# Neighbourhood attention on one Trainium2 core: slots of scores, values, transposes and fill, splits on VectorE, queries by pairs of units, shared bias tables

## The chip, the cores and the metric

The kernel runs as one program on one core of a Trainium2 chip. The core has five engines that work side by side, each through its own instructions in order: TensorE (PE in the profile) multiplies matrices and transposes, VectorE (DVE) and ScalarE (ACT) work on elements, GpSimd (POOL) too, and SyncE (SP) mostly starts transfers. Sixteen DMA engines move the data between HBM and the on-chip memory. The metric is the time of one execution on the device in microseconds; less is better. The times before the change are those of three runs, with their median.

## The reference

One layer of a hybrid encoder: an adaptive RMSNorm, a projection whose columns go to two groups of heads (2-D neighbourhood attention, and a bidirectional mLSTM), an output projection, a gated residual and a last RMSNorm. There are 2048 tokens (a grid of 32 rows and 64 columns) of width 1024, in float32. Cut to what the change touches:

```python
def rmsnorm(x, w):
    x32 = x.astype(jnp.float32)
    return x32 * lax.rsqrt(jnp.mean(x32 * x32, axis=-1, keepdims=True) + EPS) * w

def neighbourhood_attention(q, k, v, rpb):      # 8 heads of 64, window of 8 rows x 16 columns
    ...
    bias = rpb[:, dy[:, None, :, None], dx[None, :, None, :]]
    s = jnp.einsum('bhrcd,bhrjkd->bhrcjk', qg, kg).astype(jnp.float32) + bias[None]
    s = jnp.where(col_mask[:, None, :], s, -jnp.inf)
    p = jax.nn.softmax(s.reshape(B, NA_HEADS, rows, GRID_W, kh * GRID_W), axis=-1).reshape(s.shape)
    o = jnp.einsum('bhrcjk,bhrjkd->bhrcd', p, vg)
    return o.transpose(0, 2, 3, 1, 4).reshape(B, T, NA_W)
...
    na_out = neighbourhood_attention(na_q, na_k, na_v, rpb) * jax.nn.silu(na_z)
    ...
    return jnp.concatenate([na_out, ml_out], axis=-1) @ w_out
...
        h_res = h_res + gate[:, None, :] * y
    return rmsnorm(h_res, final_norm_w).astype(x.dtype)
```

## The kernel before

`phase1` and `phase1b` come first: the conditioning, the first norm, the input projection and the mLSTM. They leave queries (`d_qna`, a high and a low part), values (`d_vna`), the gate (`d_zna`), the mLSTM's output (`d_mix`), the output weights times the gate (`d_wo`) and tables of bias and mask (`d_t`) in HBM. The change touches only `phase2`, L1181 to L1500, which does the attention, the output projection and the last norm.

**Patches and units.** The grid is cut into 16 patches of 8 rows by 16 columns, 128 queries each, taken column by column, up and down in turn. A patch looks at 264 to 480 keys, by its place (edge patches at fewer, inner ones at 480). A unit is a patch and a pair of heads `ct` (0 to 3), so there are 64. Each goes through four stages:

- `stage_s`: four matmuls make the scores of two heads into `pS` (L1302 with the high part of the queries, L1303 with the low part); VectorE adds the table and takes the minimum in one instruction into `pbuf` (L1309); ScalarE takes the exponential and its sum (L1310). Behind L1309 the next table is loaded (L1274).
- `stage_n`: VectorE's reciprocal (L1319) and two multiplications, the normalisation (L1321).
- `stage_t`: TensorE transposes the probabilities into `pT` (L1331), and ScalarE copies them to `pt` (L1333).
- `stage_o`: TensorE multiplies by the values (`v` chunks of 4 or 5 grid rows) into `pO` (L1346), and VectorE multiplies by the gate, in `zs` or `gtile` by turns (L1348).

**The fill.** A generator, `outproj`, yields the 48 matmuls of a patch's output projection (L1376, into `y`), behind which VectorE adds x (L1381) and ScalarE squares (L1382). `pump(n)` takes n of them. In the first five slots the fill is what is left of the input projection (`pq`, L861). Matmuls in float32 precision go in three products of a high and a low part, so mixes and weights are split: `split_mix` and `split_w` make the high part on ScalarE (L1353, L1281) and the low part by a subtraction, most of them on GpSimd (L1354, L1282). `whi_a` and `wlo_a` hold the mixes of two patches by turns.

**The order.** It is written by hand. Slot n on TensorE is: values of unit n-2, transposes of n-1, scores of n, eight fill matmuls, four more. The normalisation of unit n is issued between the eight and the four, and is read by the transposes of the next slot. There are two `pbuf` tiles, one per head of the pair. What comes after a patch's projection (`last`: the rsqrt chain L1392 to L1178 and the scaling L1403, `store`, `load_x`) waits in the list `todo`, one entry a slot.

**The loads.** SP's queue issues tables, queries, values, gate and mixes in the order of the program; each waits for the readers of the tile that it fills, and for the SP load eight places before it, since eight semaphores go round. Queries come per patch: two of 256 KB (L1222) and two of 128 KB (L1229), at the patch's second unit, three slots ahead; one value chunk (L1243) at the third unit, the rest at the fourth, the gate (L1253) at the fourth. Tables have four buffers, two per unit. x loads (L1265) and output stores go through POOL's queue. In `phase2` SP issues 264 loads of queries, tables, values, gates and mixes: 64, 128, 40, 16 and 16.

Of the kernel before, what the change touches and what calls it, by code (L numbers as in the profile page):

```python
# [15 lines left out]
P = 128  # L16
# [7 lines left out]
NH = 8  # L24
# [34 lines left out]
class Kernel:  # L59
# [1121 lines left out]
    def phase2(self):  # L1181
# [29 lines left out]
        L = {b: {"tab": {}} for b in range(16)}  # L1211
        fnw = []

        qlow = [p.tile([P, NH, P], F32R, name=f"qlow{i}") for i in range(2)]
# [3 lines left out]
        def load_q2(b):  # L1218
            q2 = p.tile([P, NH, P], F32R, tag="q2", bufs=2, name=f"q2_{b}")
            src = self.d_qna[0, b].rearrange("(j p) c q -> p j (c q)", j=2)  # L1220
            for half in (q2[0:HD], q2[HD:P]):
                nc.sync.dma_start(half.bitcast(F32).rearrange("p (j c) q -> p j (c q)", j=2), src)  # L1222
            L[b]["q2"] = q2

        def load_ql(b):
            ql = qlow[pos[b] % 2]
            for j in range(2):
                js = slice(j * HD, (j + 1) * HD)
                nc.sync.dma_start(ql[js, 4 * j : 4 * j + 4, :].bitcast(F32), self.d_qna[1, b, js])  # L1229
            L[b]["ql"] = ql  # L1230

# [36 lines left out]
        NTAB = 4  # L1268

        def load_tab(i):  # L1270
            b, h = patches[i // 8], i % 8
            pr, pc, nr, nkc, nk, rpc, nch = geo[b]
            t = p.tile([P, 480], F32, tag="tab", bufs=NTAB, name=f"tab_{b}_{h}")
            nc.sync.dma_start(t[:, :nk], self.d_t[PR_T[pr]][PC_T[pc]][h])  # L1274
            L[b]["tab"][h] = t

# [8 lines left out]
        units = [(b, ct) for b in patches for ct in range(4)]  # L1285
        NU = len(units)
        U = {}

        def stage_s(u):
            b, ct = units[u]  # L1290
            pr, pc, nr, nkc, nk, rpc, nch = geo[b]
            lb = L[b]
# [5 lines left out]
            for j in range(2):  # L1298
# [3 lines left out]
                nc.tensor.matmul(o, lb["q2"][:, 4 * j + ct, :], kv, start=True, stop=False)  # L1302
                nc.tensor.matmul(o, lb["ql"][:, 4 * j + ct, :], kv, start=False, stop=True)  # L1303
                scores.append(ps)
            for j, ps in enumerate(scores):
                h = 2 * ct + j
                pt = pbuf[j]
                mn = p.tile([P, 1], F32, tag="mn", bufs=4, name=f"mn_{u}_{j}")
                nc.vector.tensor_tensor_reduce(pt[:, :nk], ps, lb["tab"].pop(h)[:, :nk], 1.0, 3e38, ALU.add, ALU.min, mn)  # L1309
                nc.scalar.activation(pt[:, :nk], pt[:, :nk], AF.Exp, bias=mn, scale=-1.0, accum_out=sums[:, j : j + 1])  # L1310
                pts.append(pt)
                if 2 * u + j + NTAB < 2 * NU:
# [256 lines left out]
```

## Time and profile before

| | us |
|---|---|
| median of 3 runs | 1469.06 |
| lowest, highest | 1464.5, 1472.09 |
| the profiled execution, own time | 1463.16 |
| its span in the trace | 1461.4 |
| first score matmul of the attention stage | 1020.5 |
| transposes' wait for the normalisation, in that stage | 25.5 |
| wait for values, in that stage | 17.9 |

The trace is of the profiled execution, so what is added to or taken from a time is added to 1463.16. The stage from 1020.5 to the end, some 441 us, is the one that the change touches; the first 1020 us are the same code in both kernels. "Busy" adds up the instructions' times on an engine. A window row gives for a stretch of the span the busy time and the count of each engine, then the clock granted to TensorE (1.00 is full), the mean busy share of the DMA engines, and GB/s. A row of waits reads: engine, tile and line that waited, what it waited for, total us, how many times, and the longest.

### The profile page before, as it was taken

What the parts mean: (1) busy time and instruction counts of PE and PEld (TensorE: products, weight loads), DVE (VectorE), ACT (ScalarE), POOL (GpSimd) and SP (SyncE); (2) the same over time, 40 slices, a digit from 0 to 9 for tenths busy, and PEclk for the clock granted to TensorE, in tenths of its full rate; (3) what the DMA queues carried; (4) which work ended last, traced back from release to release, by engine and by line L of the source; (5) the groups of instructions that cost most, each with busy time, mean ns of one, the idle gap of its engine ahead of it and who ended that gap; (6) DMA issues with size and microseconds to landing.
All of it is one profiled execution on the core that took longest, in us unless ns stands there. A gap on an engine that the chain in (4) does not pass through costs nothing.

```text
span 1461.4 us, 23327 instructions
## 1 busy us (share of the span) xinstructions
PE 1330.4 (91%) x8052; PEld 1133.7 (78%) x8052; DVE 791.5 (54%) x2487; ACT 527.4 (36%) x1119; POOL 285.0 (20%) x264
## 2 busy tenths in 40 slices
PE   3989998998999999999999999999779899799896
PEld 3889997998878787788788887777657677577675
DVE  6673332111464593467678787664335476466554
ACT  4633343442232232123232132223344355355451
POOL 4443122442010110012121010211141111112121
PEclk9999999999999999999999999999989899899998
DMA  9897567877285865546757669997767879697872
GB/s 317 236 287 168 127 166 204 210 180 188 68 209 135 191 186 176 144 141 181 211 182 233 210 187 272 230 244 184 244 195 171 195 183 185 176 201 180 200 180 58
DMA packets 268469, 278.99 MB, mean 191 GB/s; under 512 B 26572, under 2 KB 216780, under 8 KB 267328
## 3 DMA queue, kind: packets, MB, share of 16 engines
q1 hardware_dynamic: 187592, 219.02, 57.4%
q10 hardware_dynamic: 72328, 42.22, 10.0%
q0 software_dynamic: 8432, 16.27, 5.2%
q8 instruction: 64, 1.05, 0.3%
q14 instruction: 53, 0.43, 0.1%
HBM read 188.74 MB, written 96.92 MB: 195 GB/s over the span
## 4 chain that ended last, share of the span: by engine, by line
PE 36%; DMA 16%; DVE 6%; issue 4%; ACT 3%; SPq 1%; POOL 1%; ACTq 0%; POOLq 0%; DVEq 0%
PE pq L861 17%; PE y L1376 5%; DMA v<-d_vna 4%; PE pT L1331 2%; DMA kv<-d_ck 2%; DMA tab<-d_t 2%; DMA qlow<-d_qna 2%; ACT pbuf L1310 2%; PE pi L1070 2%; PE px L1068 2%; PE pc L425 1%; PE pc L427 1%; PE pc L426 1%; DVE pbuf L1321 1%; PE pO L1346 1%
## 5 line engine op out<-in xcount | busy, mean ns | idle before, releaser
L861 PE MATMUL pq<-hhi,whi_a 128*128 128x512 f32 x512 | 211.1, 412 | 0.8 <-ACT u L769 0.8
L861 PE MATMUL pq<-hlo,whi_a 128*128 128x512 f32 x512 | 211.7, 413 | 0.0
L861 PE MATMUL pq<-hhi,wlo_a 128*128 128x512 f32 x512 | 211.3, 413 | 0.3 <-DVE wlo_a L838 0.3
L861 PEld LDWEIGHTS pq<-hhi,whi_a 128*128 128x128 f32 x512 | 98.3, 192 | 19.5 <-ACT u L769 1.2
L861 PEld LDWEIGHTS pq<-hhi,wlo_a 128*128 128x128 f32 x512 | 98.5, 192 | 18.7 <-DVE wlo_a L838 0.7
L861 PEld LDWEIGHTS pq<-hlo,whi_a 128*128 128x128 f32 x512 | 98.2, 192 | 17.9
L1333 ACT ACTIVATE pt<-pT 96x384 f32<-96x384 f32 (+3 forms) x128 | 59.7, 512 | 116.0 <-PE pT L1331 110.2
L1310 ACT ACTIVATE pbuf<-pbuf,mn 128x480 f32<-128x480 f32 (+5 forms) x128 | 76.5, 599 | 57.6 <-DVE mn L1309 56.7
L1309 DVE CUSTOM_DVE_ANT_0 pbuf<-pS,tab 128x480 f32<-128x480 f32 (+5 forms) x128 | 65.2, 541 | 54.2 <-PE pS L1303 47.2
L1376 PE MATMUL y<-hhi,whi_a 128*128 128x512 f32 x256 | 87.1, 410 | 0.8 <-ACT whi_a L1353 0.8
L1331 PE MATMUL pT<-ident,pbuf 128*128 128x128 f32 (+2 forms) x416 | 62.5, 289 | 25.5 <-DVE pbuf L1321 25.5
L1376 PE MATMUL y<-hhi,wlo_a 128*128 128x512 f32 x256 | 84.0, 398 | 0.0
L1092 POOL TENSOR_TENSOR hm<-hm,ck 128x128 f32<-128x128 f32 x64 | 26.4, 412 | 285.3 <-DVE hm L1091 239.6
L1073 ACT ACTIVATE num<-px,gtile 128x129 f32<-128x129 f32 x120 | 38.4, 365 | 120.0 <-PE px L1068 91.8
L1346 PE MATMUL pO<-pt,v 128*64 128x128 f32 (+3 forms) x832 | 61.4, 284 | 21.8 <-DMA v<-d_vna 17.9
L425 PE MATMUL pvo<-whi_b,hhi 128*128 128x256 f32 x256 | 74.7, 292 | 7.2 <-DVE stvo L495 7.2
L1346 PEld LDWEIGHTS pO<-pt,v 128*64 128x64 f32 (+3 forms) x832 | 44.8, 138 | 46.3 <-issue 33.3
L1331 PEld LDWEIGHTS pT<-ident,pbuf 128*128 128x128 f32 (+2 forms) x416 | 45.6, 141 | 38.9 <-issue 23.0
L426 PE MATMUL pvo<-wlo_b,hhi 128*128 128x256 f32 x256 | 73.6, 288 | 0.0
L427 PE MATMUL pvo<-whi_b,hlo 128*128 128x256 f32 x256 | 73.6, 287 | 0.0
L1000 DVE TENSOR_SCALAR wv<-kv,gtile 128x129 f32<-128x129 f32 x120 | 37.3, 318 | 64.8 <-PE dc L1016 32.5
L835 POOL TENSOR_TENSOR wlo_a<-rawq,whi_a 128x1024 fp32r<-128x1024 f32 x16 | 38.5, 2409 | 159.9 <-ACT whi_a L834 139.6
(286 smaller groups left out, 3485.6 us busy)
## 6 DMA issues: line engine op xcount, KB each, us to landing
ck<-d_ck SPq DMA_DIRECT2D x64, 384.5 KB
kv<-d_ck SPq DMA_DIRECT2D x120, 128.5 KB
rawq<-in_w_main_dram SPq DMA_DIRECT2D x26, 512.0 KB
raw<-in_w_main_dram SPq DMA_DIRECT2D x20, 512.0 KB
d_ck<-stvo SPq DMA_DIRECT2D x16, 514.0 KB
x<-in_x_dram SPq DMA_DIRECT2D x16, 512.0 KB
wada<-in_w_ada_dram SPq DMA_DIRECT2D x32, 256.0 KB
dec<-d_mneg SPq DMA_DIRECT2D x32, 256.0 KB
```

The source lines that it names most:

```text
L425: nc.tensor.matmul(ps, lhi(k), rhi(k), start=(k == 0), stop=False)
L426: nc.tensor.matmul(ps, lhi(k), rlo(k), start=False, stop=False)
L427: nc.tensor.matmul(ps, llo(k), rhi(k), start=False, stop=(k == KT - 1))
L835: nc.gpsimd.tensor_tensor(lo[:, :, cs], raw, hi[:, :, cs].bitcast(F32), ALU.subtract)
L861: nc.tensor.matmul(patch_ps(ps) if patch else ps, w, self.htok(h, g, k, patch), start=(k == 0 and n == 0), stop=(k == KT - 1 and n == 2))
L1073: nc.scalar.activation(num[:, d, :], px[:, d, :], AF.Copy, scale=self.cols["inter"][:, d, h, c : c + 1])
L1309: nc.vector.tensor_tensor_reduce(pt[:, :nk], ps, lb["tab"].pop(h)[:, :nk], 1.0, 3e38, ALU.add, ALU.min, mn)
L1310: nc.scalar.activation(pt[:, :nk], pt[:, :nk], AF.Exp, bias=mn, scale=-1.0, accum_out=sums[:, j : j + 1])
L1331: nc.tensor.transpose(ps[:cs, i, :], pts[j][:, i * cs : (i + 1) * cs], self.ident)
L1333: nc.scalar.activation(t[:cs, :nch, :], ps[:cs, :nch, :], AF.Copy)
L1346: nc.tensor.matmul(po[j * HD : (j + 1) * HD, :], v[:n, h * HD : (h + 1) * HD], pt[j][:n, i, :], start=(i == 0), stop=(i == nch - 1))
L1376: nc.tensor.matmul(y, m[:, k, :], w[k][:, cs], start=(k == 4 and n == 0), stop=(k == 3 and n == 2))
```

## The change

All of it is in `phase2`:

- **Order.** A slot is now scores of unit n, values of n-2, transposes of n-1, twelve fill matmuls. The normalisation of unit n is issued behind `loads`, the rsqrt chain (`scale`, in the list `between`) ahead of it. There are four `pbuf` tiles.
- **Splits.** All low parts are made on VectorE; `mix_high` comes behind the gate's multiplication, `mix_low` behind the normalisation.
- **Queries.** They come by pairs of units into three pairs of tiles (`qhigh`, `qlow`): two loads of 128 KB and two of 64 KB, four slots ahead.
- **Tables.** Units of neighbouring patches with the same table are put next to each other by turning the order of the head pairs, and a table that is still there isn't loaded again: 108 table loads, not 128.
- **Loads spread.** At each of a patch's second and third units one value chunk, the rest at the fourth; the gate at the third; first-slot loads are put in other slots. The scaling and the store come two slots after `scale`, and the x load stands right behind the store. The last patch's end runs through its lists without a slot between.

SP then issues 308 loads in `phase2`: 128 of queries, 108 of tables, 40 of values, 16 gates and 16 mixes.

```diff
-        qlow = [p.tile([P, NH, P], F32R, name=f"qlow{i}") for i in range(2)]
+        qhigh = [p.tile([P, 2, 2, P], F32R, name=f"qhigh{i}") for i in range(3)]
+        qlow = [p.tile([P, 2, 2, P], F32R, name=f"qlow{i}") for i in range(3)]
         zs = [p.tile([P, 4, P], F32, name="zs"), self.gtile[:, 0:4]]
         chunks = {}
-        def load_q2(b):
-            q2 = p.tile([P, NH, P], F32R, tag="q2", bufs=2, name=f"q2_{b}")
-            src = self.d_qna[0, b].rearrange("(j p) c q -> p j (c q)", j=2)
-            for half in (q2[0:HD], q2[HD:P]):
-                nc.sync.dma_start(half.bitcast(F32).rearrange("p (j c) q -> p j (c q)", j=2), src)
-            L[b]["q2"] = q2
-        def load_ql(b):
-            ql = qlow[pos[b] % 2]
+        def kind(b):
+            return PR_T[b // 4], PC_T[b % 4]
+        units = []
+        for b in patches:
+            again = units and kind(b) == kind(units[-1][0])
+            order = range(4) if not units or not (again == (units[-1][1] == 3)) else range(3, -1, -1)
+            units += [(b, ct) for ct in order]
+        NU = len(units)
+        def load_q(i):
+            if 2 * i >= NU:
+                return
+            b, c0 = units[2 * i][0], min(units[2 * i][1], units[2 * i + 1][1])
+            hi, lo = qhigh[i % 3], qlow[i % 3]
+            src = self.d_qna[0, b].rearrange("(j p) c q -> p j c q", j=2)[:, :, c0 : c0 + 2]
+            for rows in (slice(0, HD), slice(HD, P)):
+                nc.sync.dma_start(hi[rows].bitcast(F32), src)
             for j in range(2):
                 js = slice(j * HD, (j + 1) * HD)
-                nc.sync.dma_start(ql[js, 4 * j : 4 * j + 4, :].bitcast(F32), self.d_qna[1, b, js])
-            L[b]["ql"] = ql
+                nc.sync.dma_start(lo[js, j].bitcast(F32), self.d_qna[1, b, js, c0 : c0 + 2])
...
-        NTAB = 4
-        def load_tab(i):
-            b, h = patches[i // 8], i % 8
-            pr, pc, nr, nkc, nk, rpc, nch = geo[b]
-            t = p.tile([P, 480], F32, tag="tab", bufs=NTAB, name=f"tab_{b}_{h}")
-            nc.sync.dma_start(t[:, :nk], self.d_t[PR_T[pr]][PC_T[pc]][h])
-            L[b]["tab"][h] = t
+        tabs = [[p.tile([P, 480], F32, name=f"tab{i}{j}") for j in range(2)] for i in range(2)]
+        place, follows, user = [], {}, {}
+        for u, (b, ct) in enumerate(units):
+            same = [w for w in (u - 1, u - 3) if w >= 0 and units[w][1] == ct and units[w][0] != b and kind(units[w][0]) == kind(b)]
+            place.append(place[same[0]] if same else (1 - place[u - 1] if u else 0))
+            if not same:
+                follows[user.get(place[u], -1 - place[u])] = u
+            user[place[u]] = u
+        def load_tab(u, j):
+            b, ct = units[u]
+            nk = geo[b][4]
+            nc.sync.dma_start(tabs[place[u]][j][:, :nk], self.d_t[PR_T[b // 4]][PC_T[b % 4]][2 * ct + j])
...
-            nc.gpsimd.tensor_tensor(wolo[k], wolo[k].bitcast(F32), wohi[k].bitcast(F32), ALU.subtract)
+            nc.vector.tensor_tensor(wolo[k], wolo[k].bitcast(F32), wohi[k].bitcast(F32), ALU.subtract)
...
-                pt = pbuf[j]
+                pt = pbuf[(2 * u + j) % 4]
...
+                if u in follows:
+                    load_tab(follows[u], j)
...
+        def mix_high(b, half):
+            nc.scalar.activation(mix_parts(b)[0][:, 4 * half : 4 * half + 4, :], mix_source(b, half), AF.Copy)
+        def mix_low(b, half):
             split.add((b, half))
             hi, lo = (part[:, 4 * half : 4 * half + 4, :] for part in mix_parts(b))
-            nc.scalar.activation(hi, src, AF.Copy)
-            eng.tensor_tensor(lo, src, hi.bitcast(F32), ALU.subtract)
+            nc.vector.tensor_tensor(lo, mix_source(b, half), hi.bitcast(F32), ALU.subtract)
...
-                    self.todo.append(lambda: store(to))
-            def store(to):
+                    self.todo += [lambda: None, store]
+            def store():
+                nc.vector.scalar_tensor_tensor(x, x, rst, fnw[0].bitcast(F32), ALU.mult, ALU.mult)
                 nc.gpsimd.dma_start(to, x)
                 if nxt is not None:
-                    self.todo += [lambda: None] * (nxt != last_b) + [lambda: load_x(nxt)]
-            self.todo += [lambda: None] * 2 * (b == b0) + [last]
+                    load_x(nxt)
+            self.between.append(scale)
...
             3: [lambda: split_w(4), lambda: split_w(5)],
-            4: [lambda: split_w(6), lambda: split_w(7)],
-            5: [lambda: load_w(0), lambda: load_w(1), lambda: load_z(b1), lambda: load_m(b1)],
-            6: [lambda: load_q2(b2), lambda: load_w(2), lambda: load_w(3), lambda: split_w(0), lambda: split_w(1)],
-            7: [lambda: load_ql(b2), lambda: load_x(b0), lambda: load_v(b2, 1), lambda: split_w(2), lambda: split_w(3)],
-            8: [lambda: load_v(b2)],
-            9: [load_fnw, lambda: load_x(b1)],
+            4: [lambda: split_w(6), lambda: split_w(7), lambda: load_x(b0)],
+            5: [lambda: load_z(b1), lambda: load_w(0), lambda: load_w(1)],
+            6: [lambda: load_m(b1), lambda: load_w(2), lambda: load_w(3), lambda: split_w(0), lambda: split_w(1), lambda: load_x(b1)],
+            7: [lambda: split_w(2), lambda: split_w(3)],
+            8: [load_fnw],
         }
         def loads(n):
             b, ct = units[n]
+            i = n % 4
             nb = after.get(b)
-            if ct == 3 and nb is not None and b != b0:
-                load_z(nb)
-            if nb is not None and b != b1:
-                if ct == 1:
-                    load_q2(nb)
-                    load_ql(nb)
-                if ct >= 2:
-                    load_v(nb, 1 if ct == 2 else 4)
+            if i % 2 == 0 and n:
+                load_q(n // 2 + 2)
+            if nb is not None and i:
+                load_v(nb, 1 if i < 3 else 4)
+                if i == 2 and b != b0:
+                    load_z(nb)
...
         def slot(n):
-            later = lambda: None
             if n == 5:
                 self.pump(max(0, self.left) + 1)
                 self.owed = 0
                 self.flush()
-                split_mix(b0, 1, zs[1], nc.vector)
+                mix_high(b0, 1)
+                mix_low(b0, 1)
                 self.queue.append(outproj(b0))
+            if n < NU:
+                stage_s(n)
+            ready = []
             if n >= 2:
                 stage_o(n - 2)
-                b, ct = units[n - 2]
-                if ct == 3 and b == b0:
-                    split_mix(b0, 0, zs[0], nc.vector)
-                elif ct == 3:
-                    later = lambda: split_mix(b, 0, zs[pos[b] % 2], nc.vector if b == last_b else nc.gpsimd)
-                elif ct == 2 and b != b0:
-                    later = lambda: (split_mix(b, 1, mix_parts(b)[1][:, 4:, :].bitcast(F32), nc.gpsimd), self.queue.append(outproj(b)))
+                b, i = units[n - 2][0], (n - 2) % 4
+                if i == 3:
+                    ready = [(b, 0)]
+                elif i == 2 and b != b0:
+                    ready = [(b, 1)]
+                    self.queue.append(outproj(b))
+            for part in ready:
+                mix_high(*part)
             if 0 <= n - 1 < NU:
                 stage_t(n - 1)
             if n < NU:
-                stage_s(n)
                 loads(n)
+            if self.between:
+                self.between.pop(0)()
+            if n < NU:
+                stage_n(n)
+            for part in ready:
+                mix_low(*part)
             for fn in first.pop(n, ()):
                 fn()
-            later()
-            rate = 22 if n < 5 else 12
-            self.pump(rate - 4)
-            if n < NU:
-                stage_n(n)
-            self.pump(4)
+            self.pump(22 if n < 5 else 12)
```

What this does to the engines' rows, at three places (a row is line, operation, output <- inputs, and the output's size). TensorE before, in the second patch column, one slot from its last value matmuls to its fill:

```order
L1346 MATMUL pO_11631<-pt_0_11586,v_2_11294 64x128
L1346 MATMUL pO_11631<-pt_1_11592,v_2_11294 64x128
L1331 MATMUL pT_0_11639<-ident,pbuf_10234 128x128 x4
L1331 MATMUL pT_1_11646<-ident,pbuf_10235 128x128 x4
L1302 MATMUL pS_0_11654<-hlo_1094,q_5_11420 128x480
L1303 MATMUL pS_0_11654<-hlo_1094,qlow_10211 128x480
L1302 MATMUL pS_1_11657<-hlo_1094,q_5_11420 128x480
L1303 MATMUL pS_1_11657<-hlo_1094,qlow_10211 128x480
L1376 MATMUL y_1_11498<-hhi_102,wlo_a 128x512 x2
L1376 MATMUL y_1_11498<-hlo_105,wlo_a 128x512
```

TensorE after, in the third column, one whole slot but for its fill:

```order
L1315 MATMUL pS_0_12185<-hhi_104,qhigh_10210 128x384
L1316 MATMUL pS_0_12185<-hhi_104,qlow_10213 128x384
L1315 MATMUL pS_1_12188<-hhi_104,qhigh_10210 128x384
L1316 MATMUL pS_1_12188<-hhi_104,qlow_10213 128x384
L1358 MATMUL pO_12197<-pt_0_12156,v_2_11656 64x128
L1358 MATMUL pO_12197<-pt_1_12162,v_2_11656 64x128
L1358 MATMUL pO_12197<-pt_0_12156,v_3_11721 64x128
L1358 MATMUL pO_12197<-pt_1_12162,v_3_11721 64x128
L1358 MATMUL pO_12197<-pt_0_12156,v_2_11911 64x128
L1358 MATMUL pO_12197<-pt_1_12162,v_2_11911 64x128
L1343 MATMUL pT_0_12205<-ident,pbuf_10244 128x128 x3
L1343 MATMUL pT_1_12211<-ident,pbuf_10245 128x128 x3
```

The scores (`pS`) stood last ahead of the fill and stand first now, so a unit's transposes (`pT`) are a slot, its scores and a values piece behind its scores.

VectorE before, from the end of an rsqrt chain (`frs`) over the scaling (L1403), the gate (L1348) and the scores (L1309) to the normalisation:

```order
L1173 SCALAR_TENSOR_TENSOR nwt_f_11820<-frs_11692,fvar_11693 128x1
L1177 TENSOR_SCALAR nwt_f_11820<-nwt_f_11820 128x1
L1178 TENSOR_TENSOR frs_11692<-frs_11692,nwt_f_11820 128x1
L1403 SCALAR_TENSOR_TENSOR xr_11502<-xr_11502,frs_11692,fnw 128x1024
L1348 TENSOR_TENSOR gtile<-pO_11831,gtile 128x128
L1309 ISA pbuf_10234,mn_0_11862<-pS_0_11856,tab_0_11732 128x480
L1309 ISA mn_0_11862 128x1
L1309 ISA pbuf_10235,mn_1_11867<-pS_1_11859,tab_1_11737 128x480
L1309 ISA mn_1_11867 128x1
L1319 RECIPROCAL sums_11855<-sums_11855 128x2
L1321 TENSOR_SCALAR pbuf_10234<-pbuf_10234,sums_11855 128x480
L1321 TENSOR_SCALAR pbuf_10235<-pbuf_10235,sums_11855 128x480
```

VectorE after, from the end of such a chain over a unit's normalisation (L1333) to the next unit's scores (L1321) and gate (L1360):

```order
L1173 SCALAR_TENSOR_TENSOR nwt_f_11728<-frs_11674,fvar_11675 128x1
L1177 TENSOR_SCALAR nwt_f_11728<-nwt_f_11728 128x1
L1178 TENSOR_TENSOR frs_11674<-frs_11674,nwt_f_11728 128x1
L1331 RECIPROCAL sums_11680<-sums_11680 128x2
L1333 TENSOR_SCALAR pbuf_10242<-pbuf_10242,sums_11680 128x480
L1333 TENSOR_SCALAR pbuf_10243<-pbuf_10243,sums_11680 128x480
L1321 ISA pbuf_10244,mn_0_11760<-pS_0_11754,tab_10217 128x480
L1321 ISA mn_0_11760 128x1
L1321 ISA pbuf_10245,mn_1_11763<-pS_1_11757,tab_10218 128x480
L1321 ISA mn_1_11763 128x1
L1360 TENSOR_TENSOR gtile<-pO_11766,gtile 128x128
```

The rsqrt chain and the scaling stood together ahead of a unit's scores; now the chain stands ahead of one unit's normalisation, and the scaling (L1426) comes behind that of the next unit, four rows further on.

SP before, from the query loads of a patch to its second value chunk:

```order
L1222 DMA q_9_11670<-d_qna 64x2x512 x2
L1229 DMA qlow_10210<-d_qna 64x512 x2
L1274 DMA tab_0_11732<-d_t_79 128x480
L1274 DMA tab_1_11737<-d_t_79 128x480
L1243 DMA v_2_11739<-d_vna 128x1x512
L1274 DMA tab_2_11792<-d_t_79 128x480
L1274 DMA tab_3_11797<-d_t_79 128x480
L1253 DMA zs<-d_zna 128x512
L1243 DMA v_3_11800<-d_vna 128x1x512
```

SP after, two units' tables, two pairs' queries and the value chunks:

```order
L1237 DMA qhigh_10210<-d_qna 64x2x256 x2
L1240 DMA qlow_10213<-d_qna 64x256 x2
L1290 DMA tab_10217<-d_t_79 128x480
L1290 DMA tab_10218<-d_t_79 128x480
L1253 DMA v_2_11656<-d_vna 128x1x512
L1237 DMA qhigh_10211<-d_qna 64x2x256 x2
L1240 DMA qlow_10214<-d_qna 64x256 x2
L1253 DMA v_3_11721<-d_vna 128x1x512
L1263 DMA zs<-d_zna 128x512
```

The four query loads of a patch became four per pair of units, each half as long, and a value chunk, a pair's queries and the gate now share the stretch in which two chunks and the gate stood.

More of the change, by code (lines that the diff above doesn't have):

```diff
@@ L1455, in phase2 @@
             self.flush()
+        self.between = []
         def slot(n):
-            later = lambda: None
             if n == 5:
@@ L1492, in phase2 @@
             while len(done) < len(patches):
-                self.step_todo()
+                while self.between:
+                    self.between.pop(0)()
+                while self.todo:
+                    self.todo.pop(0)()
                 self.pump(24)
-            while self.todo:
-                self.todo.pop(0)()
+            for fn in self.between + self.todo:
+                fn()
         pss.close()
```

41 lines of the change are left out of this document (20 added, 21 removed).

## The prediction

> **What bounds the kernel now.** I read the busy line first, then one window over the attention stage (the only part the diff touches: first score matmul at 1020.5 us, end 1461.4), then what TensorE waited for there.
>
> ```profile
> span 1461.4 us, 23327 instructions
> PE 1330.4 (91%) x8052; PEld 1133.7 (78%) x8052; DVE 791.5 (54%) x2487; ACT 527.4 (36%) x1119; POOL 285.0 (20%) x264
> 1020.00:1461.00 441.00, 376.14 (x2382) 299.13 (x2380) 232.34 (x778) 194.98 (x497) 80.25 (x70) 0.94 0.75 182
> 1119.00:1425.00 306.00, 274.84 (x1830) 220.09 (x1830) 181.01 (x619) 147.82 (x390) 51.57 (x52) 0.96 0.81 186
> PE pT L1331 <- DVE pbuf L1321: 25.5, 23, 5.9
> PE pO L1346 <- DMA v<-d_vna: 17.9, 6, 7.7
> PE pS L1303 <- DMA qlow<-d_qna: 4.9, 2, 4.4
> PE pO L1346 <- DVE gtile L1348: 3.9, 2, 2.5
> ```
>
> The window rows give busy time of TensorE, its weight loads, VectorE, ScalarE and GpSimd, then the granted clock, the DMA share and GB/s. TensorE is busy for 376.1 of 441 us; VectorE for 232.3, with room. So the order of work on TensorE and what it waits for set the stage. The waits (total, times, longest) come to 52.2 us: transposes for the normalised probabilities, values and queries for loads.
>
> A second loss hides inside TensorE's busy time:
>
> ```profile
> 1040.00:1060.00 20.00, 12.78 (x75) 10.02 (x74) 8.51 (x19) 8.48 (x20) 4.64 (x2) 0.83 0.74 239
> 1080.00:1100.00 20.00, 14.41 (x53) 10.77 (x53) 6.07 (x19) 8.55 (x17) 12.21 (x7) 0.67 0.78 213
> 1140.00:1160.00 20.00, 14.09 (x71) 11.12 (x70) 7.56 (x24) 7.92 (x21) 3.73 (x4) 0.78 0.84 192
> 1180.00:1200.00 20.00, 18.61 (x139) 14.71 (x138) 14.20 (x42) 8.73 (x21) 3.51 (x4) 1.00 0.97 205
> 1240.00:1260.00 20.00, 11.21 (x65) 9.26 (x64) 6.57 (x22) 6.28 (x17) 4.20 (x4) 0.76 0.80 188
> 1360.00:1380.00 20.00, 15.50 (x96) 12.05 (x95) 8.09 (x27) 7.76 (x21) 4.16 (x4) 0.91 0.86 207
> ```
>
> Where a long load wait falls, the granted clock is 0.67 to 0.91; where only transposes wait (1180 to 1200) it is 1.00. Busy time at share c would have been c times as long, so the loss is busy x (1 - c): 2.2 + 4.8 + 3.1 + 2.7 + 1.4 = **14 us**. It goes if the long stalls go.
>
> **Change, part 1: order of a slot, four probability buffers.** A slot of 480 keys, undisturbed (ends overlap, so I use starts):
>
> ```profile
> 1280.54 1.10 PE L1346 MATMUL pO<-pt,v 128*64 128x128 f32 x16
> 1281.57 1.14 PE L1331 MATMUL pT<-ident,pbuf 128*128 128x128 f32 x8
> 1282.47 0.47 PE L1302 MATMUL pS<-hhi,q 128*128 128x480 f32 x1
> 1283.44 0.40 PE L1376 MATMUL y<-hhi,wlo_a 128*128 128x512 f32 x1
> 1285.82 0.85 DVE L1321 TENSOR_SCALAR pbuf<-pbuf,sums 128x480 f32<-128x480 f32 x2
> 1287.31 1.09 PE L1331 MATMUL pT<-ident,pbuf 128*128 128x128 f32 x8
> 1288.16 0.47 PE L1302 MATMUL pS<-hlo,q 128*128 128x480 f32 x1
> ```
>
> Values take 1.03, transposes 0.90, scores 0.97, and the slot 5.69 (1282.47 to 1288.16). Now the transposes of a unit come 4.84 us after its scores start (1287.31 - 1282.47); its probabilities are ready at 1285.82 + 0.85 = 1286.67, so 0.64 us is spare. After the change the slot begins with the scores, and the transposes of that unit come a whole slot, a scores and a values piece later: 5.69 + 0.97 + 1.03 = 7.69 us, spare 3.5. What eats the spare today:
>
> ```profile
> 1274.30 1.90 DVE L1321 TENSOR_SCALAR pbuf<-pbuf,sums 128x480 f32<-128x480 f32 x2
> 1274.67 1.26 POOL L1354 TENSOR_TENSOR whi_a<-whi_a 128x512 fp32r<-128x512 f32 x1 [19.53 <-ACT whi_a L1353]
> 1274.91 0.63 PE L1331 MATMUL pT<-ident,pbuf 128*128 128x128 f32 x4 [1.21 <-DVE pbuf L1321]
> 1268.03 0.15 DVE L1393 TENSOR_SCALAR fvar<-fvar 128x1 f32<-128x1 f32 x1
> 1270.51 1.28 DVE L1403 SCALAR_TENSOR_TENSOR xr<-xr,frs,fnw 128x1024 f32<-128x1024 f32 x1
> ```
>
> The same two normalising instructions take 1.90 beside a GpSimd split and 0.85 without: +1.05. The rsqrt chain before L1403 takes 2.5 (1268.03 to 1270.51) and L1403 1.28. After, 2.5 stands ahead of the normalisation (spare 3.5 - 2.5 = 1.0 remains) and the 1.28 comes behind it, two slots later. Of 25.5 us I take **-24** (0 to -25.5; the short slots of the edge columns have the least spare).
>
> **Part 2: splits on VectorE.** The two shapes on that engine:
>
> ```profile
> L1354 DVE TENSOR_TENSOR whi_a<-zs,whi_a 128x512 fp32r<-128x512 f32 x1 | 0.7, 693 | 0.7 <-ACT whi_a L1353 0.7
> L838 DVE SCALAR_TENSOR_TENSOR wlo_a<-rawq,whi_a 128x1024 fp32r<-128x1024 f32 x2 | 2.5, 1225 | 8.1 <-ACT whi_a L837 8.1
> ```
>
> About 29 mix splits at 0.69 us and 8 weight splits at 1.23 move over: 20 + 10 = 30 us, VectorE then 262 of 441. I cost it at **0**: in a slot they follow the normalisation, beside the twelve fill matmuls, and the fill that reads a split's low part starts at least a slot later. Without that cover each steady split would cost up to 0.69, 20 us in all.
>
> **Part 3: loads.** Queries come in 384 KB per pair of units, four slots ahead, not 768 KB per patch at its second unit; z comes one slot earlier. Two or more value chunks of 256 KB go from "one at the third unit, the rest at the fourth" to one each at the second and third, the rest at the fourth. 20 of 128 table loads go, 4.2 MB.
>
> ```profile
> 1229.58 7.38 DMA qlow<-d_qna
> 1237.04 18.47 DMA v<-d_vna
> 1236.00:1238.00 2.00, 2.00 (x19) 1.40 (x18) 1.78 (x9) 0.00 (x0) 0.00 (x0) 1.00 1.08 177
> 1254.00:1256.00 2.00, 0.35 (x4) 0.38 (x6) 0.00 (x0) 0.00 (x0) 0.61 (x1) 0.50 0.47 124
> 1265.00:1267.00 2.00, 2.00 (x10) 1.70 (x10) 1.07 (x5) 1.59 (x5) 0.00 (x0) 1.00 0.42 103
> q1 hardware_dynamic: 38058, 59.97, 54.5%
> ```
>
> In the chain of waits the last value chunk before a new column lands 18.47 us after its issue, begun with the DMA share at 1.08 in a burst of queries, values and z; at 1265 the share is 0.42. So bursts, not the mean (0.81), make values late. 54.5% of 441 us for 59.97 MB is 4.0 us of all sixteen DMA engines per MB. At a column change three chunks are new and the last is issued no earlier than now, but behind less. Tables aside, the loads from the patch's second unit up to and with it are 768 + 256 + 256 + 512 = 1792 KB now; after, 256 + (384 + 256 + 256) + 256 = 1408, as half of the queries go ahead of the burst. Of the fourth unit's own loads it waits behind 256 KB (a chunk) less. 384 + 256 KB are 0.64 MB, or 2.6 us. Its deadline is 1 us later too (scores go first). The 7.7 us stall becomes 4 to 5; the other five, 10.2 us together, 2.0 each, mostly go; inside a column the last chunk is a slot (4.7 to 5.7 us) earlier. Values: **-12** (0 to -17.9). Queries -4 (0 to -4.9); z (the 3.9 us on L1348 stands behind its load) -3 (0 to -3.9). The tables' 17 us of DMA time is worth nothing to TensorE by itself. With most of the stalls most of the clock loss goes: **-9** (0 to -14).
>
> **Part 4: costs.** The first slots put 384 KB more queries ahead of the last in-projection weights, +2 (0 to +3, by the page's 4.0 us per MB). At the end nothing follows to hide the last splits and the last x load:
>
> ```profile
> 1430.41 0.88 PE L1346 MATMUL pO<-pt,v 96*64 96x128 f32 x12 [1.45 <-DVE gtile L1348]
> 1446.87 0.69 DVE L1381 TENSOR_TENSOR xr<-xr,y 128x512 f32<-128x512 f32 x1 [2.75 <-PE y L1376]
> ```
>
> The wait of 1.45 goes, and the last x load is issued about 3 us later, with its sum at 1446.87 still some 10 us off: +1 (-1.5 to +2).
>
> **Sum:** -24 - 12 - 4 - 3 - 9 + 2 + 1 = -49. The profiled execution took 1463.2 us (span 1461.4), so 1414; the median before, 1469.06, lies 5.9 above that execution, so I predict **1417**, between 1414 and 1420.
>
> **Rivals.** *Loads still bind.* If a value load is slow for itself, not by the burst, spreading does little. For it: at 1254 to 1256 TensorE waits for values while the share is only 0.47. Against: inside a column the load starts a slot earlier anyway. Then only part 1 and the costs count: -24 + 3 = -21, 1442 own, about **1445**.
> The Trainium skill ("DMA: Bandwidth & Descriptors", section "Why a DMA increments its semaphore by 16 and not by 1") has a rule for this: a DMA runs on the largest k up to 16 that divides the slowest dimension of both sides. A value load reads 4 or 5 grid rows, so by it 4 or 5 of 16 engines would move it, unchanged by the diff. The row at 1254 fits the rule, the row at 1236 (all sixteen full) says the burst is enough; by the rule the sum is this rival's.
>
> *All load waits vanish.* -25.5 - 17.9 - 4.9 - 3.9 - 14 = -66, costs hidden: 1397 own, **1400**. Undisturbed slots (5.69 at 480 keys) say TensorE could do it; against it, the first slots keep their burst of weights.
>
> *The number of loads binds (slower).* Each SP load also waits for the load eight before it, since eight semaphores go round. Loads per patch in SP's queue rise from 16.5 (264 over 16) to 19.25 (308); a patch takes 306 / 13 = 23.5 us. It decides once the mean landing exceeds 8 x 23.5 / 19.25 = 9.8 us. If before's loads already filled the lanes (8 x 23.5 / 16.5 = 11.4), a patch would take 27.4: 13 x 3.9 = +51, less 24: 1490 own, about **1494**.
>
> ```profile
> SPq L1274 <- DVE mn L1309: 167.6, 73, 9.4
> SPq L1274 <- DMA tab<-d_t: 15.4, 15, 3.0
> 797.21 5.07 DMA kv<-d_ck
> 809.53 4.04 DMA zt<-d_zml
> ```
>
> For it speaks the landing of 18.47; against, that SP waits 167.6 us for table readers and 15.4 for other loads.
> The Trainium skill (same page, section "Bandwidth") says to batch DMAs to 1 MiB and that transfers under 64 KB pay mostly overhead, which speaks against 128 and 64 KB queries. The rows above agree that size isn't what sets a landing (128 KB in 5.07, 256 KB in 4.04).
>
> *The waits only move.* The rsqrt chain now stands ahead of the normalisation, the splits behind; if the spare of 3.5 us is used up by a late VectorE, most transposes' waits return: 1463 own, no change. VectorE's 262 of 441 us speaks against.
>
> **How the numbers follow.** Forecast (1405 to 1430) 0.52; loads still bind 0.20; all vanish 0.18; waits only move 0.05; slower 0.05. The range takes in the forecast and the first two rivals: 1395 to 1447. Half a percent, 7.3 us, is about what can be told from no change. Faster by more: 0.91; within: 0.04; slower: 0.05.
>
> **What would show it.** After: waits of the transposes for normalised probabilities near zero outside the first slots; every steady slot of 480 keys at 5.7 us; two normalising instructions at 0.85 always; waits for values near 6 us, none over 5; granted clock above 0.9 in every window from 1119 on; splits on VectorE with TensorE never waiting for a low part; SP's waits on other loads near 15 us. It is wrong if the values' waits stay at 18, or if SP waits long on queries.

## The result, and the profile after

| | before | after | ratio, with its 95% interval |
|---|---|---|---|
| with the prediction's result | 1469.55 us | 1420.33 us | 0.9687 (0.9627 to 0.9748) |
| the changed kernel once more (first set below) | 1467.66 us | 1428.24 us | 0.9736 (0.9684 to 0.9787) |
| and again (last set below) | 1461.23 us | 1421.50 us | 0.9733 (0.9702 to 0.9764) |

So the change makes the kernel about 2.6 to 3.1% faster; 1417 was predicted, in 1395 to 1447. The times are medians of all executions; the ratio is taken over those in the chip's faster state, and so isn't quite that of the medians. The profiled execution of the changed kernel took 1432.65 us and was the slowest of its four, so its own difference, 1463.2 - 1432.7 = 30.5 us, is smaller than that of the medians (49). The third row's profiled execution took 1419.3.

The page's first lines and windows of the changed kernel; columns as before (busy TensorE, weight loads, VectorE, ScalarE, GpSimd, clock, DMA share, GB/s):

```profile
span 1430.9 us, 23354 instructions
PE 1323.5 (92%) x8052; PEld 1129.2 (79%) x8052; DVE 802.1 (56%) x2524; ACT 521.8 (36%) x1119; POOL 228.3 (16%) x230
1060.00:1080.00 20.00, 11.87 (x65) 9.46 (x65) 8.08 (x21) 6.65 (x16) 0.71 (x1) 0.74 0.82 192
1180.00:1200.00 20.00, 20.00 (x148) 16.10 (x147) 11.83 (x36) 10.92 (x28) 1.18 (x2) 1.00 0.85 190
1240.00:1260.00 20.00, 18.10 (x112) 14.10 (x113) 12.64 (x44) 9.24 (x26) 1.18 (x2) 0.94 0.78 202
1119.00:1390.00 271.00, 260.42 (x1747) 210.90 (x1746) 178.21 (x611) 135.03 (x366) 14.16 (x24) 0.98 0.77 187
```

From 1119 to 1390 TensorE is busy for 96% of the time (before, 90% from 1119 to 1425). Over the whole stage it is idle for 38.1 us (64.9 before), and its busy time, for the same matmuls, is 373.8 us (376.1 before). What it still waits for in the stage, and what VectorE and SyncE's queue wait for (total, times, longest):

```profile
PE pO L1358 <- ACT pt L1345: 9.3, 8, 2.3
PE y L1395 <- ACT whi_a L1368: 7.9, 1, 7.9
PE y L1395 <- ACT hhi L1296: 2.3, 1, 2.3
PE pT L1343 <- DVE pbuf L1333: 1.5, 2, 1.0
DVE pbuf L1321 <- DMA tab<-d_t: 28.0, 16, 5.6
SPq L1290 <- DVE mn L1321: 55.5, 29, 8.7
SPq L1290 <- DMA v<-d_vna: 20.8, 7, 4.4
SPq L1263 <- DMA v<-d_vna: 11.3, 4, 4.6
```

The kernel before, for the tables and for the longest of the queue's waits for values:

```profile
DVE pbuf L1309 <- DMA tab<-d_t: 5.3, 5, 3.0
SPq L1229 <- DMA v<-d_vna: 11.2, 3, 5.1
```

The transposes hardly wait now, and nothing on TensorE waits for values, queries or z by name. But **VectorE now waits 28.0 us for tables** (5.3 before), and SyncE's queue waits for value loads: over all its lines up to 1400 us, 51.4 us in 22 waits, against 18.5 in 6 before. Up to there it waits 106.3 us for other transfers of any kind, against 52.8. Its waits for VectorE to finish reading a table, which were time to spare, fell from 162.8 to 55.5 us. One place, at a new column, shows how that reaches TensorE (start, duration; in brackets the idle time before it and its releaser), in rows of the timeline of SyncE's queue, VectorE, ScalarE and TensorE:

```profile
1233.25 0.56 SPq L1253 DMA_DIRECT2D v<-d_vna  x1
...
1239.52 0.56 SPq L1253 DMA_DIRECT2D v<-d_vna  x1
1244.70 0.32 SPq L1263 DMA_DIRECT2D gtile<-d_zna  x1
1245.46 2.82 SPq L1290 DMA_DIRECT2D tab<-d_t  x4
...
1253.59 0.66 DVE L1321 CUSTOM_DVE_ANT_0 pbuf<-pS,tab 128x480 f32<-128x480 f32 x1 [3.01 <-DMA tab<-d_t]
...
1254.29 0.70 ACT L1322 ACTIVATE pbuf<-pbuf,mn 128x480 f32<-128x480 f32 x1 [5.32 <-DVE mn L1321]
1256.18 1.06 ACT L1345 ACTIVATE pt<-pT 128x512 f32<-128x512 f32 x2
...
1256.81 2.05 PE L1358 MATMUL pO<-pt,v 128*64 128x128 f32 x16 [1.79 <-ACT pt L1345]
```

The queue stands from 1240 to 1244.7 before a gate load, for a value load in flight (the 4.6 us of the row above): the one eight loads before it, issued at 1233.25. The tables behind the gate go out from 1245.5 on, and the first that VectorE needs has arrived by 1253.6, so the table is late by the queue's stand and by some 8 us of its own in flight. The table is added late, ScalarE's exponential waits for that, and the copies (`pt`) of the unit before stand behind the exponential in ScalarE's order. So TensorE waits for `pt`, and the cause is a load. The longest of these waits, 2.3 us at 1168, looks different and is the same. VectorE idles 4.96 us there, put down to scores of TensorE, but these were done at 1159.5. That leaves the table, whose load went out at 1154.9:

```profile
1159.13 0.38 PE L1316 MATMUL pS<-hhi,qlow 128*128 128x480 f32 x1
1164.38 0.66 DVE L1321 CUSTOM_DVE_ANT_0 pbuf<-pS,tab 128x480 f32<-128x480 f32 x1 [4.96 <-PE pS L1315]
1168.15 2.13 PE L1358 MATMUL pO<-pt,v 128*64 128x128 f32 x16 [2.34 <-ACT pt L1345]
```

The steady slot is as the prediction drew it:

```profile
1191.60 0.39 PE L1315 MATMUL pS<-hhi,qhigh 128*128 128x480 f32 x1
1194.84 0.85 DVE L1333 TENSOR_SCALAR pbuf<-pbuf,sums 128x480 f32<-128x480 f32 x2
1197.30 0.38 PE L1315 MATMUL pS<-hlo,qhigh 128*128 128x480 f32 x1
1199.30 1.09 PE L1343 MATMUL pT<-ident,pbuf 128*128 128x128 f32 x8
```

The pitch is 5.70 (1191.60 to 1197.30), and the transposes start 7.70 us after the scores of their unit; 7.69 was worked out.

### The profile page after: what moved, and what is told of

Its sections match the earlier page's. It is cut to its first block, busy times and chain, and to the rows that moved or that the text cites. A ratio compares the mean times of both kernels' runs of the same rounds, so it can differ in the third digit from the quotient of the medians.

```text
span 1430.9 us, 23354 instructions
## 1 busy us (share of the span) xinstructions
PE 1323.5 (92%) x8052; PEld 1129.2 (79%) x8052; DVE 802.1 (56%) x2524; ACT 521.8 (36%) x1119; POOL 228.3 (16%) x230
## 4 chain that ended last, share of the span: by engine, by line
PE 40%; DMA 15%; issue 6%; DVE 2%; ACT 2%; POOL 1%; SPq 1%; POOLq 0%; ACTq 0%; DVEq 0%
PE pq L861 15%; PE y L1395 8%; DMA tab<-d_t 4%; PE pT L1343 3%; PE pO L1358 3%; DMA qhigh<-d_qna 2%; DMA ck<-d_ck 2%; DMA v<-d_vna 2%; DMA kv<-d_ck 2%; PE pc L425 2%; PE pc L427 2%; PE pc L426 2%; PE pi L1070 1%; PE px L1068 1%; PE dc L1016 1%
## 5 line engine op out<-in xcount | busy, mean ns | idle before, releaser
L1321 DVE CUSTOM_DVE_ANT_0 pbuf<-pS,tab 128x480 f32<-128x480 f32 (+5 forms) x128 | 65.4, 541 | 59.7 <-DMA tab<-d_t 28.0
L1395 PE MATMUL y<-hhi,whi_a 128*128 128x512 f32 x256 | 88.2, 414 | 10.2 <-ACT whi_a L1368 7.9
L710 ACT ACTIVATE dec<-dec,gtile 128x128 f32<-128x128 f32 x128 | 42.0, 392 | 71.9 <-POOL dec L706 69.0
L495 DVE TENSOR_TENSOR stvo<-pvo,brow 128x256 f32<-128x256 f32 x64 | 26.5, 421 | 73.8 <-PE pvo L427 60.0
L1395 PEld LDWEIGHTS y<-hhi,whi_a 128*128 128x128 f32 x256 | 49.5, 197 | 20.3 <-ACT whi_a L1368 8.2
```

Of the source, the lines that this page charges most:

```text
L710: nc.scalar.activation(t[:, d, o, :], t[:, d, o, :], AF.Exp, bias=self.cols["g"][:, d, h, c : c + 1])
L1321: nc.vector.tensor_tensor_reduce(pt[:, :nk], ps, tabs[place[u]][j][:, :nk], 1.0, 3e38, ALU.add, ALU.min, mn)
L1395: nc.tensor.matmul(y, m[:, k, :], w[k][:, cs], start=(k == 4 and n == 0), stop=(k == 3 and n == 2))
```

## The experiments

Each ratio is to the kernel before, run on the same chip. "The stage" is the time from the first score matmul to the end of the span, in the profiled execution: 440.9 us before; 411.9, 404.6 and 408.2 in the three profiles of the changed kernel, so single profiles of one kernel differ by up to 7 us. The interval of a ratio reaches some 0.4% to each side, so two runs of different sets can be told apart from about 0.6%, 9 us, on.

**The changed kernel again.**

> The changed kernel once more, as the reference of this set. Ratio to the kernel before 0.965 to 0.972 (about 1418 to 1428 us). In the trace: transposes wait under 3 us for the normalisation; VectorE waits some 28 us for tables, and values wait some 9 us for the copies of the transposes, where tables came late.

Ratio 0.9736, just outside what was expected. Values wait 4.5 us for the copies (some 9 expected) and VectorE 21.5 us for tables (some 28), so these waits change by that much from one execution to the next; the transposes wait 1.0.

**Parts of the change.** First the loads, tables, scaling and stores alone (the comments stand for the rest of the edit):

```diff
-        pbuf = [... for i in range(4)]      # slot: scores, values, transposes; low parts on nc.vector
+        pbuf = [... for i in range(2)]      # slot: values, transposes, scores; low parts on nc.gpsimd
```

> The changed kernel with the old order of a slot, two probability buffers and the low parts on GpSimd again: only the loads, tables, scaling and stores as changed. Theory (the loads brought about half): transposes wait some 25 us for the normalisation as before, waits for values and queries under 5 us together: 1440 to 1450 us. Rival (the loads brought nothing, late tables took it back): 1460 to 1470 us.

1452.24 us, ratio 0.9895 (0.985 to 0.994), stage 424.5. The time lies just above the theory's range. The gain is real but a third to two fifths of the whole. Transposes wait less than the 25 us expected, and values more:

```profile
PE pT L1343 <- DVE pbuf L1333: 17.0, 12, 5.9
PE pO L1358 <- DMA v<-d_vna: 10.6, 4, 5.1
```

Then order and loads, with only the splits put back:

```diff
-            nc.vector.tensor_tensor(lo, mix_source(b, half), hi.bitcast(F32), ALU.subtract)
+            (nc.vector if b in (b0, last_b) else nc.gpsimd).tensor_tensor(lo, mix_source(b, half), hi.bitcast(F32), ALU.subtract)
```

> The changed kernel with the low parts on GpSimd again. Theory (the order of the slot removes the transposes' waits, with 3.5 us to spare): transposes wait under 5 us, 1418 to 1427 us. Rival (GpSimd's splits beside the normalisation were the cause): 15 to 20 us of waits come back, 1435 to 1445 us.

1422.71 us, ratio 0.972 (0.9666 to 0.9774), stage 403.8: the theory, and as the changed kernel. GpSimd's splits still slow the normalisation, but TensorE has no wait of the transposes left. The group of the normalisation's instructions of 480 keys, in this run (busy total and mean ns of one):

```profile
L1333 DVE TENSOR_SCALAR pbuf<-pbuf,sums 128x480 f32<-128x480 f32 x32 | 18.1, 608 | 0.6
```

and in the changed kernel:

```profile
L1333 DVE TENSOR_SCALAR pbuf<-pbuf,sums 128x480 f32<-128x480 f32 x32 | 13.6, 468 | 0.6
```

And the splits alone, on the kernel before:

```diff
-            nc.gpsimd.tensor_tensor(wolo[k], wolo[k].bitcast(F32), wohi[k].bitcast(F32), ALU.subtract)
+            nc.vector.tensor_tensor(wolo[k], wolo[k].bitcast(F32), wohi[k].bitcast(F32), ALU.subtract)
...
-                    later = lambda: split_mix(b, 0, zs[pos[b] % 2], nc.vector if b == last_b else nc.gpsimd)
+                    later = lambda: split_mix(b, 0, zs[pos[b] % 2], nc.vector)
```

> The kernel before with all low parts on VectorE and nothing else. Theory (they are one cause of several): transposes' waits fall by 5 to 12 us, 1457 to 1466 us. Rival (they are the main cause): by 20 us or more, 1445 to 1450 us. Second rival (the splits on VectorE push the normalisation back as much as the contention did): no change, 1466 to 1473 us.

1453.9 us, ratio 0.9915 (0.9883 to 0.9948), stage 432.8. The time lies between the ranges of the theory and of its first rival, and the mechanism is neither's. TensorE's waits:

```profile
PE pT L1331 <- DVE pbuf L1321: 39.4, 22, 4.5
PE pO L1346 <- DMA v<-d_vna: 4.4, 2, 2.3
```

and VectorE's timeline at one split:

```profile
1190.84 0.69 DVE L1354 TENSOR_TENSOR wlo_a<-wlo_a 128x512 fp32r<-128x512 f32 x1 [1.48 <-ACT wlo_a L1353]
1191.64 0.85 DVE L1321 TENSOR_SCALAR pbuf<-pbuf,sums 128x480 f32<-128x480 f32 x2
```

The transposes wait 14 us longer than before, as the split now stands ahead of the normalisation and itself waits for ScalarE; the loads' waits fall by about as much. So TensorE is idle for 64.3 us of the stage, as before (64.9). What falls is its busy time, from 376.1 to 368.5 us for the same matmuls: by the prediction's sum over windows of 20 us, the granted clock costs 10.7 us and not 17.3. The longest wait for values is 2.3 us where it was 7.7. That shorter waits are what kept the clock up fits these rows but was not tested. The waits of one kernel do not add up like costs: time lost at a transpose is time in which a load arrives.

**The late tables.** ScalarE's and VectorE's order first, with the additions and exponentials of a unit moved behind the copies of the one before:

```diff
-            if n < NU:
-                stage_s(n)
+            soft = stage_s(n) if n < NU else lambda: None      # soft: table, minimum, exponential
...
                 stage_t(n - 1)
+            soft()
```

> The changed kernel, with the table additions and exponentials of unit n issued behind the gate of n-2 and the copies of n-1 instead of ahead of them. Theory (late tables reach TensorE because ScalarE's copies and VectorE's gate stand behind the unit that waits for its table): values' waits for the copies and for VectorE fall from 5 to 9 us to under 2, and the time by 3 to 8 us against the changed kernel (ratio to the kernel before 0.962 to 0.970). Rival (the loads are late as a whole, so the wait only moves to the transposes or to the values' loads): within 0.3% of the changed kernel, ratio 0.969 to 0.974.

1429.89 us, ratio 0.9749 (0.970 to 0.9798), stage 411.1: the rival, a little above its range. Nothing waits for the copies any longer, but TensorE waits for values' loads (6.1 us), at the scores (5.9) and at the transposes (3.9). That fits loads that are late as a whole, where the order chooses who waits.

Then the value loads on GpSimd's queue:

```diff
-                    nc.sync.dma_start(chunks[key][: n * nkc, :], ...)
+                    nc.gpsimd.dma_start(chunks[key][: n * nkc, :], ...)
...
-                    load_x(nxt)
+                    self.todo += [lambda: None, lambda: load_x(nxt)]
```

> The changed kernel with the 40 value loads on GpSimd's queue instead of SyncE's, and the x load two slots behind the store, so that they don't stand behind it. Theory (eight loads in flight on SyncE's queue, slow value loads among them, make the tables late): SyncE's waits for other loads fall from 95 to 106 us to under 60, VectorE's for tables from 21 to 28 us to under 10, ratio 0.958 to 0.968. Rival (the DMA engines' bandwidth makes tables late, whatever the queue): VectorE still waits over 15 us for tables, or values wait for their loads; ratio 0.969 to 0.976.

1413.29 us, ratio 0.9637 (0.9591 to 0.9683), stage 390.2. It is faster than the changed kernel. SyncE's waits for other transfers fall to about 60 us (without a last wait of 32 us, that of the closing store for an x load, behind which no load stands), but VectorE's for tables hardly:

```profile
DVE pbuf L1321 <- DMA tab<-d_t: 25.5, 14, 6.8
PE pO L1358 <- ACT pt L1345: 3.3, 2, 2.3
```

So the theory holds for the time, and nearly for the queue. VectorE's table waits, which it had under 10 us, are what the rival asks (over 15); what reaches TensorE by the copies went from 9.3 to 3.3 us. Another 5 us lie in the first slots: the wait for the mixes' high part, 7.7 to 8.2 us in the three profiles of the changed kernel, is 3.1 here. The second edit, x two slots later, was not tried by itself.

**Bytes or number of loads.** Sharing of tables undone:

```diff
-            same = [w for w in (u - 1, u - 3) if ...]
+            same = []
```

> The changed kernel, loading every table again (128 loads, not 108). Theory (20 more loads in a full queue, 17 us more of DMA time): VectorE waits 5 to 15 us longer for tables, the time rises by 3 to 10 us, ratio 0.974 to 0.981. Rival (sharing is worth nothing): within 0.3% of the changed kernel.

1437.04 us, ratio 0.9814 (0.9772 to 0.9857), stage 418.5: sharing is worth some 0.8%, 12 us, with 4 to 20 left open by the intervals. VectorE's table waits are 35.8 us. The same edit with the value loads on GpSimd's queue:

> Value loads on GpSimd's queue, and every table loaded (128 loads): the bytes of unshared tables where SyncE's queue has 20 loads fewer than in the changed kernel. If the number of loads counts: within 4 us of the values on that queue with shared tables, ratio 0.962 to 0.968. If the bytes count: 7 to 12 us slower than that, ratio 0.968 to 0.974.

1405.09 us, ratio 0.9632 (0.9597 to 0.9666), stage 391.2: no loss that can be told against 0.9637 and 390.2. The same 4.2 MB cost some 12 us where SyncE's queue holds 328 loads, and nothing, give or take 8, where it holds 288. That points to the queue and away from the bytes, but the two costs differ by little more than their errors. The queue's waits aren't the measure of it either: for other transfers they are 26 us longer than with the values alone on that queue (without the closing store), and the time isn't.

A direct test, 20 loads of 8 KB in place of the shared tables:

```diff
+                elif u < NU - 2:
+                    nc.sync.dma_start(spare, self.d_t[...][...][2 * ct + j][:, :16])
```

> The changed kernel with 20 loads of 8 KB into a tile that nothing reads, on SyncE's queue, where a shared table isn't loaded: the number of loads of unshared tables without their bytes. Theory (the number of loads in flight counts): 4 to 9 us slower than the reference of this set, ratio up by 0.003 to 0.006, and SyncE's waits for other loads rise. Rival (the bytes count): within 3 us of the reference.

1444.22 us, ratio 0.9905 (0.9868 to 0.9942): 23 us slower than the reference, far more than either theory. My test was flawed: all 20 fill one tile and go out in pairs, so the second waits for the first to land, with SyncE's queue behind it:

```profile
SPq L1328 <- DMA spare<-d_t: 61.9, 11, 8.4
```

It shows what holding that queue for 62 us costs, and not what a load in flight costs. Even 8 KB took up to 8.4 us to land there.

**Where values and gates are issued.**

```diff
-            if nb is not None and i:
-                load_v(nb, 1 if i < 3 else 4)
-                if i == 2 and b != b0:
-                    load_z(nb)
+            if nb is not None and i and (i > 1 or b == b0):
+                if i == 3 and b != b0:
+                    load_z(nb)
+                load_v(nb, 1 if i < 3 else 4)
```

> The changed kernel with the value chunks and the gate issued where they were: one chunk at the third unit, gate and the rest at the fourth. Theory (the earlier, spread issue is what removed the waits for values): waits for values of 5 to 12 us come back, 4 to 12 us slower than the changed kernel, ratio 0.974 to 0.982. Rival (the queries by pairs alone relieved the burst): within 0.3%.

1426.25 us, ratio 0.9728 (0.9685 to 0.9771): the rival, no change that can be told. The waits for values come back as the theory asks, and the time does not, as the copies' wait goes:

```profile
PE pO L1358 <- DMA v<-d_vna: 8.9, 5, 4.4
PE pO L1358 <- ACT pt L1345: 0.8, 2, 0.5
```

**The reference, and the furthest version.**

> The changed kernel again, as the reference of this set: ratio to the kernel before 0.966 to 0.976.

Ratio 0.9733, as expected. With gates and mixes on GpSimd's queue as well as values:

```diff
-            nc.sync.dma_start(zs[pos[b] % 2], self.d_zna[b])
+            nc.gpsimd.dma_start(zs[pos[b] % 2], self.d_zna[b])
...
-            nc.sync.dma_start(mix_parts(b)[1][:, 4:, :].bitcast(F32), self.d_mix[b])
+            nc.gpsimd.dma_start(mix_parts(b)[1][:, 4:, :].bitcast(F32), self.d_mix[b])
```

> Values, gates and mixes on GpSimd's queue (72 loads less on SyncE's). If SyncE's loads in flight still make tables late: VectorE's waits for tables fall below 15 us, ratio 0.955 to 0.962. If what remains is the DMA engines' burst at a new column: no gain over the values alone, 0.961 to 0.968, or a loss where gates stand behind the stores that wait for the scaling.

1405.49 us, ratio 0.9616 (0.9589 to 0.9644), stage 395.3, where the two expectations overlap. Here too x comes two slots later. VectorE's table waits are 23.5 us, and 9.7 of them stand at the very first unit, whose scores came early, at 1008.9:

```profile
DVE pbuf L1321 <- DMA tab<-d_t: 23.5, 14, 9.7
1017.29 0.46 DVE L1321 CUSTOM_DVE_ANT_0 pbuf<-pS,tab 128x288 f32<-128x288 f32 x1 [9.74 <-DMA tab<-d_t]
```

Behind that unit they are 13.8, under the 15 that the queue theory asks, and the copies' wait is 0.2 us. The time beats both kernels, but can't be told from the values alone.

## Why the prediction was right, point by point

| term | predicted, us | measured, us (first and third profile of the changed kernel) |
|---|---|---|
| transposes' waits | -24 | 25.5 to 1.5 and 1.0: -24.0 and -24.5 |
| values' waits | -12 | 17.9 to 0, but 9.5 and 8.3 for the copies and VectorE, 8.2 and 7.0 of it behind late tables: -8 and -10 |
| queries, z | -4, -3 | 4.9 and 3.9 to 0 |
| clock | -9 | 17.3 to 12.3 and 10.4, summed over windows of 20 us from the first score matmul on: -5 and -7 |
| first slots | +2 | five kinds of waits, 14.2 and 13.4 in place of 1.3: about +13 and +12 |
| end | +1 | last values to the end 31.0 before, 31.2 after: 0 |
| sum | -49 | -33 and -38 by these rows; the stage itself -29.0 and -32.7 |

- **The number: near, and partly by luck.** The sum of 49 us is what the first set shows between its medians (1469.55 to 1420.33), but the two larger sets show 39 and 40, and the stage's profiles 29 to 36. The forecast of 1417 came within 4 us of the result with one cost, the first slots, 10 us too small and with two gains, values and clock, 4 to 8 us too large between them. The profiles show less than the medians at least in part because the one profile of the kernel before is of an execution (1463.2) faster than all four of the first set.
- **Order of the slot: right in mechanism and size.** The spare of 3.5 us held, also behind the rsqrt chain. Order and four buffers on top of the loads are worth 1.8% (ratio 0.9895 to 0.972). Without the new loads they were not run.
- **Splits at nothing: right** given the new order (0.972 against 0.9733). On the kernel before they are worth 0.85%, in TensorE's busy time and not in its waits.
- **Loads: the size held, the step did not.** "Spreading" values and gate a slot earlier was to bring most of 12 us and brought none that can be told (0.9728 without it): 8.9 us of waits for values moved to the copies. "The tables' 17 us of DMA time is worth nothing to TensorE by itself" was wrong: some 12 us hang on the 20 loads saved. The runs point to SyncE's queue as the limit, in which a load stands behind the one eight places before it: with 40 value loads elsewhere the kernel gains 1%, and the 20 loads cost nothing that shows. That tables then come on time was not shown; VectorE waits 25.5 us for them still. The rival that named it ("the number of loads binds") did not come out as a slower kernel, but its mechanism was at work: the queue's waits for other transfers went from 52.8 to 106.3 us (95.9 and 98.4 in the other two profiles). That the saved tables paid for part of the added query loads is my reading. The prediction took 15.4 us of waits of one line as evidence against it; the sum over all lines, 52.8, would have been the number to read.
- **First slots: undersized.** In slot 5 the first output projection waits 7.9 us for the mixes' high part, which stands on ScalarE behind the last eviction of queries:

```profile
1066.19 0.69 ACT L885 ACTIVATE qst<-pq,bcol 128x512 fp32r<-128x512 f32 x1 [5.41 <-DMA d_qna<-qst]
1068.11 0.63 ACT L1368 ACTIVATE whi_a<-gtile 128x512 fp32r<-128x512 f32 x1 [1.23 <-DVE qst L886]
1068.79 0.80 PE L1395 MATMUL y<-hhi,whi_a 128*128 128x512 f32 x1 [7.94 <-ACT whi_a L1368]
```

The eviction is put down to a store of queries, and two such stores go out on ScalarE's own queue just ahead of it, from 1063.90 to 1066.09, though ScalarE is free from 1060.8 on. Why they go out so late isn't settled, and no run was made for it. With the values on GpSimd's queue two stores go out at 1055.19 and 1056.40, and the wait is 3.1 us, so the loads seem to have a part in it.
- **"All load waits vanish"** did not happen: 7 to 8 us stay behind late tables.
- **Signs that failed.** The clock was to stay above 0.9 in every window from 1119 on. It is 0.94 at a new column in the first profile, but 0.83 in a window at 1160 in the second and 0.86 at 1140 in the third. SyncE's waits for other loads were to stay near 15 us. The steady slot, the normalisation and the transposes came out as drawn.

Open: whether a value load is slow for itself (few DMA engines, by the rule of the Trainium skill that the prediction weighed, "DMA: Bandwidth & Descriptors", section "Why a DMA increments its semaphore by 16 and not by 1") or by its company. With the values on GpSimd's queue, 256 KB of values took a median of 10.2 us from issue to landing, and 512 KB of x 9.3, so size doesn't set it there; how many engines carried them the trace doesn't show.

## What to carry to other kernels

Put a stage's producer a whole slot ahead of its consumer on the bounding engine before you shave the instructions between them: 3.5 us of spare made both the rsqrt chain and the contention free. When loads bind, look at what the issuing queue waits for, over all lines, and not at bytes alone; moving 40 loads to a second queue (with x later) was worth another 1%. And follow a wait back through the engines' orders: "waits for a copy" was a late table.

## What was not expected of the hardware

A normalising instruction of 480 keys takes 721 ns on average in the kernel before, and 468 where nothing but the splits has moved from GpSimd to VectorE. The first 1020 us, the same code in every kernel, end between 1006.3 and 1025.0 us in the profiles, so two executions can differ by up to 19 us before the changed stage begins; the stage by itself is steadier (404.6 to 411.9 us in three profiles of one kernel).
